# Order of the passes over a split weight granule: both passes on the high half first, those on the low half last

## The chip, the cores and the metric

The kernel runs on one core of one Trainium2 chip. The metric is device time in microseconds (us), median of several runs. TensorE (PE, with its weight loads PEld), VectorE (DVE), ScalarE (ACT), GpSimd (POOL) and SyncE (SP, which here only issues DMAs) each work through a queue of their own and wait for each other by semaphores.

## The reference, cut to what matters

One decoder layer on 512 tokens of width 2048, all in float32. The large matrix products are `h @ w_in` (2048 x 6160), `o @ w_o` (2048 x 2048), the FFN's up projection `h @ w_ffn_in` (2048 x 11264) and its down projection (5632 x 2048):

```python
h = rmsnorm(x, attn_pre_norm[l])
m = token_mixer(h, w_in[l], ...)          # proj = h @ w_in; GLA heads and differential attention; o @ w_o
x = x + rmsnorm(m, attn_post_norm[l])
h = rmsnorm(x, ffn_pre_norm[l])
f = conv_ffn(h, w_ffn_in[l], ...)         # up = h @ w_ffn_in; (gelu(conv(a)) * b) @ w_ffn_out
x = x + rmsnorm(f, ffn_post_norm[l])
```

## The kernel before

**Split operands.** Each operand X of a large product is held as two tiles of a reduced type: a high half (`hi`, X rounded by an ACT copy) and a low half (`lo` = X - hi, a DVE subtraction). A product is then three matmuls: high tokens by high weights, low tokens by high weights, high tokens by low weights. Token halves lie in `ah` and `al` (or in `in_s2h`, `in_s2l` and the like for sums of token blocks).

**Granules.** Weights come in granules of 128 x 1024 elements: a DMA brings one into a buffer (`raw` or `rt`, four of each; `wt`), ACT writes the high half (line 137), DVE the low half (line 138), each into one of three slots of `ring` (some granules go to other tiles, `xhi` and `xlo`, or to `w`). A granule feeds 24 matmuls with 256 columns or 12 with 512 columns. The high slot is written again when the last matmul that reads it is done, and so is the low slot; the buffer is loaded again when the DVE subtraction is done.

**Stages.** In order of time: the boot with the first input projection (`first_half`, then `proj_n` and `proj_t`); the mixer, whose input projections run in `InUnit`, with the matmuls of the heads (GLA and attention, plain float32, made by generators that `step()` moves on) between granules; the output projection (`proj_n`, `to_ffn`); the up projection (`up_prods`, in units of seven block products after a Strassen-like scheme); the down projection (`down_prods`, ten units, each of seven block products of two granules); and the last group of 512 rows (`last_group`, `ffn_out_part`).

- `mm_n` (lines 191 to 193): one token tile by two slices of a granule; tokens are loaded as the stationary operand, weights move (512 columns). It is called for four token tiles in turn per granule.
- `InUnit.run` (lines 742 to 744 and 746 to 748): either weights are stationary and tokens move (`turned`), or the other way round; 256 columns.
- `down_prods` (lines 1349 to 1351): token sums stationary, weights move, 512 columns, two banks `b[0]` and `b[1]` for the two token tiles. When a block product is done, `into` adds each bank to `acc` (line 1357, DVE; line 1355, ACT, for a first one). The same banks are written on by a later block product.
- `ffn_out_part` (lines 1553 to 1555), in the last group; `mm_t` (lines 173 to 175) and `up_prods` (lines 1247 to 1249) have moving tokens and stay as they are.

**What sets the order.** In `first_half`, `to_ffn`, `run_in_order` (the change from up to down projection) and the end of `last_group` PE, ACT, DVE and POOL run in the order of the code. Elsewhere a list scheduler, which plays the program through with a model of time, sets the order of each engine, DMA queues included. So a change in the order of PE's code can move other engines' instructions there.

In a down unit the weights of three blocks are loaded from memory, others are made from them: `more` (line 1195, POOL) adds a second block to a buffer by an accumulating DMA, and lines 1212 and 1230 (DVE) add one buffer to another. Token sums are loaded into `st` and split by lines 150 and 151.

## Time and profile before

| | |
|---|---|
| median of 3 runs | 2100.62 us (2098.62 to 2102.5) |
| the profiled execution's own time | 2097.49 us |
| its span, first to last instruction | 2095.8 us |
| mean granted TensorE clock | 0.998 |
| DVE busy | 1509.7 us, 72% of the span |
| ACT busy | 1002.5 us, 48% |
| POOL busy | 286.3 us, 14% |
| DMA, mean | 171 GB/s |

In the profile's rows `L1350 PE MATMUL bank<-ring,ah` names line, engine, operation, and output and inputs (moving operand first). A row of waits reads: engine, tile and line that waited, what it waited for, then the time in total, how often, and the longest one. A matmul's end is modelled, so that matmuls that follow each other overlap in the rows: their rate is read from the starts.

### The profile page before, as it was taken

What the parts mean: (1) busy time and instruction counts of PE and PEld (TensorE: products, weight loads), DVE (VectorE), ACT (ScalarE), POOL (GpSimd) and SP (SyncE); (2) the same over time, 40 slices, a digit from 0 to 9 for tenths busy, and PEclk for the clock granted to TensorE, in tenths of its full rate; (3) what the DMA queues carried; (4) which work ended last, traced back from release to release, by engine and by line L of the source; (5) the groups of instructions that cost most, each with busy time, mean ns of one, the idle gap of its engine ahead of it and who ended that gap; (6) DMA issues with size and microseconds to landing.
All of it is one profiled execution on the core that took longest, in us unless ns stands there. A gap on an engine that the chain in (4) does not pass through costs nothing.

```text
span 2095.8 us, 35570 instructions
## 1 busy us (share of the span) xinstructions
PE 2059.0 (98%) x14449; PEld 1900.7 (91%) x14449; DVE 1509.7 (72%) x1802; ACT 1002.5 (48%) x1306; POOL 286.3 (14%) x306
## 2 busy tenths in 40 slices
PE   7999999999999999999999999999999999999997
PEld 6699999999988889899999999999999878787786
DVE  5967777676762255976777777777777778888877
ACT  5544444455742233454554554555455554444443
POOL 0112222322200000011011111110111110110100
PEclk9999999999999999999999999999999999999999
DMA  5488887878884344447667577667766876776763
GB/s 210 121 186 182 193 193 177 180 176 196 197 229 151 96 159 151 138 107 192 153 150 192 144 162 186 142 160 173 167 157 181 240 211 166 189 195 159 175 166 141
DMA packets 280696, 358.60 MB, mean 171 GB/s; under 512 B 14592, under 2 KB 221876, under 8 KB 278612
## 3 DMA queue, kind: packets, MB, share of 16 engines
q1 hardware_dynamic: 191380, 259.85, 37.2%
q0 software_dynamic: 84800, 94.38, 29.7%
q8 instruction: 113, 1.85, 0.4%
q10 hardware_dynamic: 4352, 2.10, 0.3%
q14 instruction: 51, 0.42, 0.1%
HBM read 311.72 MB, written 44.56 MB: 170 GB/s over the span
## 4 chain that ended last, share of the span: by engine, by line
PE 60%; issue 30%; DMA 3%; DVE 3%; POOL 3%; ACT 1%; SPq 0%; POOLq 0%; DVEq 0%; ACTq 0%
PE bank L1247 6%; PE bank L1248 6%; PE bank L1249 6%; PE bank L192 3%; PE bank L193 3%; PE bank L191 3%; PE bank L742 3%; PE bank L744 3%; PE bank L743 3%; PE bank L746 3%; PE bank L748 3%; PE bank L747 3%; PE bank L173 2%; PE bank L175 2%; PE bank L174 2%
## 5 line engine op out<-in xcount | busy, mean ns | idle before, releaser
L138 DVE TENSOR_TENSOR ring<-raw,ring 128x1024 fp32r<-128x1024 f32 x315 | 383.4, 1222 | 281.0 <-ACT ring L137 271.1
L137 ACT ACTIVATE ring<-raw 128x1024 fp32r<-128x1024 f32 x315 | 333.2, 1060 | 509.2 <-PE bank L1248 113.9
L1247 PE MATMUL bank<-ah,ring 128*128 128x256 f32 x1280 | 353.4, 276 | 0.0
L1248 PE MATMUL bank<-al,ring 128*128 128x256 f32 x1280 | 353.4, 276 | 0.0
L1249 PE MATMUL bank<-ah,ring 128*128 128x256 f32 x1280 | 353.4, 276 | 0.0
L137 ACT ACTIVATE ring<-rt 128x1024 fp32r<-128x1024 f32 x221 | 233.4, 1060 | 247.8 <-PE bank L1248 154.9
L138 DVE TENSOR_TENSOR ring<-rt,ring 128x1024 fp32r<-128x1024 f32 x221 | 269.1, 1221 | 86.9 <-ACT ring L137 86.7
L1247 PEld LDWEIGHTS bank<-ah,ring 128*128 128x128 f32 x1280 | 240.3, 188 | 0.1
L1248 PEld LDWEIGHTS bank<-al,ring 128*128 128x128 f32 x1280 | 240.3, 188 | 0.1
L1249 PEld LDWEIGHTS bank<-ah,ring 128*128 128x128 f32 x1280 | 240.3, 188 | 0.0
L1350 PE MATMUL bank<-ring,ah 128*128 128x512 f32 x424 | 166.2, 392 | 6.3 <-DVE ring L138 6.3
L1351 PE MATMUL bank<-ring,al 128*128 128x512 f32 x424 | 165.1, 389 | 0.0
L1349 PE MATMUL bank<-ring,ah 128*128 128x512 f32 x424 | 158.3, 391 | 0.0
L192 PE MATMUL bank<-ring,ah 128*128 128x512 f32 x280 | 110.0, 394 | 0.6 <-DVE ring L138 0.6
L191 PE MATMUL bank<-ring,ah 128*128 128x512 f32 x280 | 109.6, 397 | 0.0
L193 PE MATMUL bank<-ring,al 128*128 128x512 f32 x280 | 109.3, 393 | 0.0
L1195 POOL DMA_DIRECT2D raw<-in_w_ffn_in_dram x40 | 51.2, 1309 | 395.5 <-DVE ring L138 395.5
L1350 PEld LDWEIGHTS bank<-ring,ah 128*128 128x128 f32 x424 | 79.6, 188 | 26.1 <-DVE ring L138 9.9
L1349 PEld LDWEIGHTS bank<-ring,ah 128*128 128x128 f32 x424 | 79.5, 188 | 18.1 <-ACT ring L137 1.4
L1195 POOL DMA_DIRECT2D rt<-in_w_ffn_in_dram x40 | 50.9, 1271 | 326.9 <-DVE ring L138 292.4
L1351 PEld LDWEIGHTS bank<-ring,al 128*128 128x128 f32 x424 | 79.6, 188 | 16.3
L746 PE MATMUL bank<-ring,ah 128*128 128x256 f32 x320 | 92.7, 290 | 1.7 <-ACT ring L137 1.0
(346 smaller groups left out, 5670.9 us busy)
## 6 DMA issues: line engine op xcount, KB each, us to landing
raw<-in_w_ffn_in_dram SPq DMA_DIRECT2D x96, 512.0 KB, 5.0
raw<-in_w_in_dram SPq DMA_DIRECT2D x56, 512.0 KB, 4.8
raw<-in_w_ffn_out_dram SPq DMA_DIRECT2D x48, 512.0 KB, 6.2
raw<-in_w_in_dram POOLq DMA_DIRECT2D x40, 512.0 KB, 7.1
rt<-in_w_ffn_in_dram SPq DMA_DIRECT2D x40, 512.0 KB, 5.6
rt<-in_w_ffn_in_dram POOLq DMA_DIRECT2D x40, 512.0 KB, 6.1
raw<-in_w_ffn_in_dram POOLq DMA_DIRECT2D x40, 512.0 KB, 6.8
raw<-in_w_o_dram SPq DMA_DIRECT2D x32, 512.0 KB, 3.9
```

The source lines that it names most:

```text
L137: act(hi, raw, AF.Copy)
L138: tt(lo, raw, hi.bitcast(F32), ALU.subtract)
L191: mm(banks[t], ah[:, t, s, :], w[0][:, k, :], start=st, stop=False)
L192: mm(banks[t], ah[:, t, s, :], w[1][:, k, :], start=False, stop=False)
L193: mm(banks[t], al[:, t, s, :], w[0][:, k, :], start=False, stop=sp)
L746: mm(o, sh[:, n, kk, :], wh[:, k, :], start=st, stop=False, **NOW)
L1247: mm(o, wh, sh[:, :, kk, :], start=start and kk == 0 and n == 0, stop=False, **NOW)
L1248: mm(o, wh, sl[:, :, kk, :], start=False, stop=False, **NOW)
L1249: mm(o, wl, sh[:, :, kk, :], start=False, stop=kk == HK - 1, **NOW)
L1349: mm(b[j], sh[:, o:o + P], w[0][:, q, :], start=start and st == 0, stop=False, **NOW)
L1350: mm(b[j], sh[:, o:o + P], w[1][:, q, :], start=False, stop=False, **NOW)
L1351: mm(b[j], sl[:, o:o + P], w[0][:, q, :], start=False, stop=st == 3, **NOW)
```

## The change

Within each granule, all matmuls that read the high half of the weights come first, and those that read the low half last. Before, the three products of one slice followed each other. This is done in `InUnit.run`, in `down_prods`, in `ffn_out_part` and in `mm_n`; in `mm_n` within the six matmuls of one token tile only. The matmuls themselves, their number, operands and banks stay the same.

```diff
     def mm_n(banks, t, g, w, slots=tuple(range(KT))):
-        for k in range(2):
+        for v, p, k in ((ah, 0, 0), (al, 0, 0), (ah, 0, 1), (al, 0, 1), (ah, 1, 0), (ah, 1, 1)):
             i = 2 * g + k
-            st, sp, s = i == 0, i == KT - 1, slots[i]
-            mm(banks[t], ah[:, t, s, :], w[0][:, k, :], start=st, stop=False)
-            mm(banks[t], ah[:, t, s, :], w[1][:, k, :], start=False, stop=False)
-            mm(banks[t], al[:, t, s, :], w[0][:, k, :], start=False, stop=sp)
+            mm(banks[t], v[:, t, slots[i], :], w[p][:, k, :], start=i == 0 and p == 0 and v is ah,
+               stop=i == KT - 1 and p == 1)
...
                 wh, wl = granule(None, 4, raws[g])
-                for n in range(2):
-                    o = b[:, 256 * n:256 * (n + 1)]
-                    for k in range(4):
-                        kk = 4 * g + k
...
-                            mm(o2, ch, sh[:, :, kk, :], start=st, stop=False, **NOW)
-                            mm(o2, ch, sl[:, :, kk, :], start=False, stop=False, **NOW)
-                            mm(o2, cl, sh[:, :, kk, :], start=False, stop=sp_, **NOW)
-                        else:
-                            mm(o, sh[:, n, kk, :], wh[:, k, :], start=st, stop=False, **NOW)
-                            mm(o, sl[:, n, kk, :], wh[:, k, :], start=False, stop=False, **NOW)
-                            mm(o, sh[:, n, kk, :], wl[:, k, :], start=False, stop=sp_, **NOW)
+                for w in (wh, wl):
+                    for n in range(2):
+                        o = b[:, 256 * n:256 * (n + 1)]
+                        for k in range(4):
+                            kk = 4 * g + k
...
+                                mm(o2, cw, sh[:, :, kk, :], start=st, stop=sp_, **NOW)
+                                if w is wh:
+                                    mm(o2, cw, sl[:, :, kk, :], start=False, stop=False, **NOW)
+                            else:
+                                mm(o, sh[:, n, kk, :], w[:, k, :], start=st, stop=sp_, **NOW)
+                                if w is wh:
+                                    mm(o, sl[:, n, kk, :], w[:, k, :], start=False, stop=False, **NOW)
...
     def down_prods(b, op, g, w, start):
         sh, sl = (piece(v, *place[op]) for v in (ah, al))
-        for j in range(2):
-            for q in range(2):
-                o = 512 * g + 256 * q + P * j
-                st = 2 * g + q
-                mm(b[j], sh[:, o:o + P], w[0][:, q, :], start=start and st == 0, stop=False, **NOW)
-                mm(b[j], sh[:, o:o + P], w[1][:, q, :], start=False, stop=False, **NOW)
-                mm(b[j], sl[:, o:o + P], w[0][:, q, :], start=False, stop=st == 3, **NOW)
+        for p in range(2):
+            for j in range(2):
+                for q in range(2):
+                    o = 512 * g + 256 * q + P * j
+                    st = 2 * g + q
+                    mm(b[j], sh[:, o:o + P], w[p][:, q, :], start=start and st == 0 and p == 0,
+                       stop=st == 3 and p == 1, **NOW)
+                    if p == 0:
+                        mm(b[j], sl[:, o:o + P], w[0][:, q, :], start=False, stop=False, **NOW)
...
     def ffn_out_part(us, gr, t, c):
         b = bank()
-        for k in range(4):
...
-            mm(b, uh[:, tk], hi[:, k % 2, :], start=k == 0, stop=False)
-            mm(b, uh[:, tk], lo[:, k % 2, :], start=False, stop=False)
-            mm(b, ul[:, tk], hi[:, k % 2, :], start=False, stop=k == 3)
+        for v, p, k in [(v, 0, k) for k in range(4) for v in range(2)] + [(0, 1, k) for k in range(4)]:
+            mm(b, us[k][v][:, tk], gr[k // 2][p][:, k % 2, :], start=(v, p, k) == (0, 0, 0),
+               stop=(p, k) == (1, 3))
```

Lines 195 to 730 of the kernel before stand two lines higher in the changed one, `into` two lines lower, `ffn_out_part` and what follows one line higher.

**PE, one granule of a down unit.** Before (in square brackets the engine whose semaphore the instruction waits for; ACT writes the high half, DVE the low one):

```order
L1349 MATMUL bank<-ring,ah 128x512 [waits Activation_49]
L1350 MATMUL bank<-ring,ah 128x512 [waits DVE_49]
L1351 MATMUL bank<-ring,al 128x512
L1349 MATMUL bank<-ring,ah 128x512
L1350 MATMUL bank<-ring,ah 128x512
L1351 MATMUL bank<-ring,al 128x512
L1349 MATMUL bank<-ring,ah 128x512
L1350 MATMUL bank<-ring,ah 128x512
L1351 MATMUL bank<-ring,al 128x512
L1349 MATMUL bank<-ring,ah 128x512
L1350 MATMUL bank<-ring,ah 128x512
L1351 MATMUL bank<-ring,al 128x512
```

And in the changed kernel, where line 1350 multiplies high tokens (by either half of the weights) and line 1353 low tokens:

```order
L1350 MATMUL bank<-ring,ah 128x512 [waits Activation_49]
L1353 MATMUL bank<-ring,al 128x512
L1350 MATMUL bank<-ring,ah 128x512
L1353 MATMUL bank<-ring,al 128x512
L1350 MATMUL bank<-ring,ah 128x512
L1353 MATMUL bank<-ring,al 128x512
L1350 MATMUL bank<-ring,ah 128x512
L1353 MATMUL bank<-ring,al 128x512
L1350 MATMUL bank<-ring,ah 128x512 [waits DVE_49]
L1350 MATMUL bank<-ring,ah 128x512 x3
```

The wait for DVE's low half moved from the second matmul of the granule to the ninth; the twelve matmuls are the same.

**DVE in a down unit**, where the scheduler sets the order: line 138 is a low half of weights, line 151 a low half of token sums, line 1357 (1359 in the changed kernel) adds a finished bank to `acc`. Before:

```order
L151 TENSOR_TENSOR al<-st,ah 128x1024
L138 TENSOR_TENSOR ring<-raw,ring 128x1024 x2
L1357 TENSOR_TENSOR acc_16858<-acc_16858,bank 128x512
L1357 TENSOR_TENSOR acc_16859<-acc_16859,bank 128x512
L151 TENSOR_TENSOR al<-st,ah 128x1024
L138 TENSOR_TENSOR xlo<-raw,xhi 128x1024
```

And in the changed kernel:

```order
L138 TENSOR_TENSOR ring<-raw,ring 128x1024
L151 TENSOR_TENSOR al<-st,ah 128x1024
L138 TENSOR_TENSOR ring<-raw,ring 128x1024
L1359 TENSOR_TENSOR acc_16858<-acc_16858,bank 128x512
L1359 TENSOR_TENSOR acc_16859<-acc_16859,bank 128x512
L138 TENSOR_TENSOR xlo<-raw,xhi 128x1024
L151 TENSOR_TENSOR al<-st,ah 128x1024
```

A low half of weights moved ahead of the low half of token sums that stood before it.

**SP, which issues the loads**, at the change from one group of down units to the next (before with -, changed with +; `st` are token sums, `raw` and `rt` weights):

```order
-L102 DMA raw<-in_w_ffn_out_dram 128x2x512
+L102 DMA raw<-in_w_ffn_out_dram 128x2x512 x2
 L48 DMA st<-sd2a_8344 128x1024
 L102 DMA raw<-in_w_ffn_out_dram 128x2x512 x2
 L48 DMA st<-sd3a_8349 128x1024
-L102 DMA raw<-in_w_ffn_out_dram 128x2x512
 L48 DMA st<-sd3s_8352 128x1024
-L48 DMA rt<-in_w_ffn_out_dram 128x2x512
+L48 DMA rt<-in_w_ffn_out_dram 128x2x512 x2
 L48 DMA st<-sd3s_8353 128x1024
-L48 DMA rt<-in_w_ffn_out_dram 128x2x512
```

The weight loads `raw` and `rt` each stand one load of token sums earlier than before.

In the mixer too DVE, ACT and, in a few places, SP and POOL have a changed order of the heads' work against the weight splits. In the up projection, up to the change to the down projection, no engine's order is changed.

13 lines of the change are left out of this document (6 added, 7 removed).

## The prediction

> **What bounds the kernel now.** I read the clock first, then the page's busy shares, the list of waits of PE, and the stages.
>
> ```profile
> core 0: 2095.8 us, clock 0.998
> PE 2059.0 (98%) x14449; PEld 1900.7 (91%) x14449; DVE 1509.7 (72%) x1802; ACT 1002.5 (48%) x1306; POOL 286.3 (14%) x306
> ```
>
> PE is busy for 98% of the span at full clock. Its matmuls are neither fewer nor smaller afterwards, so the change can win only some of the 36.8 us in which PE is idle, plus what the modelled ends hide. The list of PE's waits says which part:
>
> ```profile
> PE bank L158 <- DVE xt L247: 10.4, 2, 9.5
> PE bank L1350 <- DVE ring L138: 6.3, 8, 1.0
> PE bank L1350 <- DVE xlo L138: 1.6, 3, 0.8
> PE bank L646 <- ACT aT L639: 1.3, 1, 1.3
> PE bank L646 <- DMA dvt<-dvd: 1.0, 1, 1.0
> PE bank L746 <- ACT ring L137: 1.0, 1, 1.0
> PE bank L175 <- DVE xlo L138: 0.8, 1, 0.8
> PE bank L1554 <- DVE xlo L138: 0.8, 1, 0.8
> PE bank L748 <- DVE ring L138: 0.8, 1, 0.8
> PE bank L192 <- DVE ring L138: 0.6, 1, 0.6
> ```
>
> Every row with `L138` is PE waiting for a low half. Except for L175, which the change leaves alone, they are matmuls that read the low half: L1350 (down projection, 11 times, 7.9 us), L1554, L748 and L192 (once each). The 10.4 us of L158 are the boot's wait for scaled tokens. PE meets its low half almost at once after the high one; in the timeline of the down stage:
>
> ```profile
> 1820.37 0.39 PE L1351 MATMUL bank<-ring,al 128*128 128x512 f32 x1
> 1820.59 0.62 PE L1349 MATMUL bank<-ring,ah 128*128 128x512 f32 x2
> 1822.24 0.50 PE L1350 MATMUL bank<-ring,ah 128*128 128x512 f32 x1 [1.03 <-DVE ring L138]
> 1822.58 0.39 PE L1351 MATMUL bank<-ring,al 128*128 128x512 f32 x1
> ```
>
> From start to start a 512-column matmul takes 0.22 us (1820.37 to 1820.59), so the second of the two L1349 began at about 1820.82, and the low half was 1.2 us late (1822.24 less 1820.82, less 0.22).
>
> **The change, part by part.**
>
> *Down projection, the wait for the low half.* How much later may the low half come? Before, it is the second matmul of a granule, afterwards the ninth: seven matmuls of 0.227 us, 1.6 us later. The longest wait listed for it is 1.0 us, the one above 1.2 us by its starts. So all 11 waits should go. What each is worth is more than its listed idle time, since the modelled end covers a part. A second place, with the cause in view (PE, ACT and DVE):
>
> ```profile
> 1692.36 0.39 PE L1351 MATMUL bank<-xhi,al 128*128 128x512 f32 x1
> 1692.62 0.50 PE L1349 MATMUL bank<-ring,ah 128*128 128x512 f32 x1
> 1693.88 0.50 PE L1350 MATMUL bank<-ring,ah 128*128 128x512 f32 x1 [0.76 <-DVE ring L138]
> 1694.22 0.39 PE L1351 MATMUL bank<-ring,al 128*128 128x512 f32 x1
> 1696.61 0.51 PE L1349 MATMUL bank<-ring,ah 128*128 128x512 f32 x1
> 1697.86 0.50 PE L1350 MATMUL bank<-ring,ah 128*128 128x512 f32 x1 [0.75 <-DVE ring L138]
> ...
> 1691.50 1.06 ACT L137 ACTIVATE ring<-rt 128x1024 fp32r<-128x1024 f32 x1 [8.48 <-PE bank L1351]
> 1695.49 2.01 ACT L137 ACTIVATE ring<-rt 128x1024 fp32r<-128x1024 f32 x2 [1.01 <-DMA rt<-in_w_ffn_out_dram]
> ...
> 1692.60 1.23 DVE L138 TENSOR_TENSOR ring<-rt,ring 128x1024 fp32r<-128x1024 f32 x1 [5.30 <-ACT ring L137]
> ```
>
> L1349 to L1350 takes 1.26 us in place of 0.23, and the next step 0.34: 1.14 us lost where 0.76 us of idle time is listed. In the first example it is 1.2 + 0.1 for 1.03. With 0.3 us more for each, the 11 waits are worth 7.9 + 11 x 0.3 = 11.2 us.
>
> Not all of it stays won, since the high half is late here too: ACT begins when the accumulating DMA into `rt` lands, ends at 1692.56, and PE begins at 1692.62. The granule behind it starts at 1696.61, 0.33 us after its predecessor, again right behind its own high half. That DMA is issued once, so when the first of the pair loses its 1.1 us stall, PE reaches the second 1.1 us earlier and waits for the high half. I take 1.0 us off for this pair. The other pairs that I see in the timeline lie several granules apart, and there the load chain begins with a ring slot that PE frees, so it moves with PE. The weight loads name the granules in which the high half is just in time:
>
> ```profile
> PEld bank L1350 <- DVE ring L138: 9.9, 10, 1.5
> PEld bank L1350 <- DVE xlo L138: 3.1, 4, 1.1
> PEld bank L1349 <- ACT ring L137: 1.4, 4, 0.5
> ```
>
> Four granules. The low slot is now read by the twelfth matmul, not by the eleventh, so DVE gets it back 0.23 us later, and with it comes the next load of that buffer: 4 x 0.23 = 0.9 us off. The high slot comes free four matmuls (0.9 us) earlier, which I count as nothing, since ACT is busy for less than half of the time. Down projection: 11.2 - 1.0 - 0.9 = 9.3 us.
>
> *The two banks.* The first bank's last matmul moves from sixth to tenth of the last granule, 0.9 us later; the second bank still ends with the twelfth. DVE adds the two to `acc` one behind the other, and stands still if it comes too early, with the next low half behind it.
>
> ```profile
> L1357 DVE TENSOR_TENSOR acc<-acc,bank 128x512 f32<-128x512 f32 x124 | 80.8, 679 | 3.1 <-PE bank L1351 3.1
> 1645.00:2035.00 390.00, 382.03 (x1688) 311.89 (x1687) 322.44 (x341) 182.20 (x190) 44.97 (x38) 1.00 0.71 188
> ```
>
> In 124 such additions DVE waited for PE for 3.1 us in all, so it nearly always comes after both banks are done. If it comes exactly when the second is done less its 0.68 us for the first, the first may now hold it by 0.23 us (0.68 less two matmuls). DVE has 390 - 322 = 68 us free in this stage. I cost it at nothing; the cover is the 1.6 us that a low half may now be late. If it is gone, see the second rival.
>
> *Order of DVE and SP.* Weight halves go ahead of token halves on DVE (one operation, 1.22 us by the row of 1692.60), and the weight loads one `st` load earlier on SP. The latter bears on the late high halves, since SP is a queue:
>
> ```profile
> SPq L48 <- DVE al L151: 155.1, 35, 13.1
> ```
>
> A load of token sums that waits for its buffer holds the weights behind it. I see no granule whose lateness this row proves, so I take nothing; at best the late high halves go (1.9 us more), at worst a token half comes 1.22 us later and PE waits for it. No wait of PE above names `al` of L151; were token halves late as often as weights are (11 waits in 10 units of 14 granules), 35 splits would give 3 waits of 1.1 us, 3 us.
>
> *Last group, mixer, projections.* L1554: 0.8 + 0.3 = 1.1 us; the low half may be 1.6 us later, so it goes. L748: the low half moves from third to seventeenth of 24 matmuls of 0.113 us, 1.6 us later, so 0.8 + 0.2 = 1.0 us goes; L746, which waited 1.0 us for the high half right before it, stays. L192: `mm_n` orders only its own six matmuls, so the low half is allowed just 3 x 0.227 = 0.7 us more, against 0.6 + 0.3 = 0.9 us: I take 0.7.
>
> *The reordered mixer.* The scheduler moves the heads' work among the weight splits. Where PE idles there:
>
> ```profile
> 400.00:620.00 220.00, 214.63 (x1654) 202.94 (x1653) 154.21 (x285) 130.29 (x246) 43.67 (x55) 0.99 0.81 192
> ```
>
> 5.4 us, of which 1.0 is L746 and 0.8 L748. Of the other 3.6 us, 2.3 are attention's (L646). No row shows what the new order does to it; I bound it by all 3.6 us gone and by the 5.4 us doubled, and take 0, because the same work fills the same gaps.
>
> *Reloading weights.* The loads show whether the order of operands on PE matters by itself:
>
> ```profile
> L1350 PEld LDWEIGHTS bank<-ring,ah 128*128 128x128 f32 x424 | 79.6, 188 | 26.1 <-DVE ring L138 9.9
> L1351 PEld LDWEIGHTS bank<-ring,al 128*128 128x128 f32 x424 | 79.6, 188 | 16.3
> ```
>
> Before, L1349 and L1350 mostly use the same stationary tile in turn; afterwards they don't. The row of L1350 has a load of 188 ns for each of its matmuls, as L1351, whose tile is new each time. So nothing is saved before, and nothing lost after: 0. The Trainium skill ("TensorE: Matmul & The Clock Gate", section "Step-by-step: what each phase is for") says that loading and multiplying are separate so that one can load once and multiply repeatedly; by that rule this change would give up reuse. The trace doesn't agree that any is had here (188 ns on both rows).
>
> *Sum.* 9.3 + 1.1 + 1.0 + 0.7 = 12.1 us off the profiled execution: 2097.5 (span 2095.8 and 1.7 around it) less 12.1 is 2085.4. That execution lies 3.1 us under the median of the runs, 2100.6, so the forecast as a median is 2088.5 us.
>
> **The rivals.**
>
> *The stalls move to the high half (no change).* Every late granule is late because its buffer landed late, and PE, coming earlier, waits on L137 in place of L138. For it speaks the pair at 1692 and 1696; against it, that only four weight loads waited for a high half, and that ACT elsewhere is ahead by whole granules: in the first example it was DVE that was behind. Then only L1554, L748 and the second half of L192's stay won, about 2.5 us: 2098 us.
>
> *DVE held by the banks (slower).* At the end of each of the 70 block products of the down projection DVE stands 0.23 us longer before the first bank, and the low halves behind it come late by more than their 1.6 us. It decides once DVE's backlog eats that cover, so if DVE comes to the additions early. The price is 70 x 0.23 = 16 us at the most, and the 11.2 us of stalls stay as they are: 2100.6 - 2.8 (the other places) + 16 = 2114 at worst, and half of it 2106. Against it: 3.1 us of such waits in all, 68 us of free time.
>
> *The mixer's new order costs (less gain).* The doubled 5.4 us against the sum: 2094 us.
>
> *Reuse lost.* If a matmul whose stationary tile is the one before's needed no load of its own, 560 pairs in the down projection (10 units x 14 granules x 4) would each get one more load of 188 ns, all of it exposed at worst: 105 us, 2088.5 + 105 = 2194 us. The equal 188 ns rows leave it 1 in 100. (It is the rule of the Trainium skill's page named above.)
>
> **How the numbers follow.** Chances: the forecast, with the stalls gone (2083 to 2092), 0.64; the mixer's loss or part of the stalls moved (2092 to 2096), 0.15; stalls moved whole (2097 to 2100), 0.14; slower, 0.07, of which 0.06 is DVE held and 0.01 reuse. The lower end of the range is the forecast with the mixer's 3.6 us and the late high halves' 1.9 us won too: 2088.5 - 5.5 = 2083. The upper end takes in the moved stalls: 2100. A measurement tells about 0.2%, 4.2 us, from no change, so faster is below 2096.4: 0.79; within 0.2%: 0.14; slower: 0.07.
>
> **What would show it.** Right: no waits for DVE in the down stage's matmuls (lines 1350 and 1353 then), nor in the last group's or the mixer's L746 to L748; PE's busy time unchanged at the same rate of 0.227 and 0.113 us; idle time of PE below 25 us. A high half in place of the low one in the list of waits (ACT L137 or its DMA) would show the first rival, additions to `acc` that wait for PE the second, weight loads of other than 188 ns the last. The forecast is wrong if the gain of the down stage is under 5 us, or if the mixer's stretch from 400 to 620 us moves by more than 5 us.

## The result, and the profile after

The changed kernel is slower: 2109.74 us in the median of 5 runs (2105.51 to 2111.13) against 2100.62 us (5 runs, 2098.62 to 2104.17). The ratio is 1.0039, with a 95% interval of 1.0023 to 1.0054: 8 us more (5 to 11), where 12 us less were forecast. Both signs by which the forecast was to be called wrong came true: the down stage gained less than 5 us, and the mixer moved by more. The profiled execution took 2109.98 us:

```profile
core 0: 2108.3 us, clock 0.996
```

```profile
PE 2063.5 (98%) x14449; PEld 1906.8 (90%) x14449; DVE 1507.1 (71%) x1802; ACT 999.7 (47%) x1306; POOL 281.4 (13%) x306
```

The work is the same (14449 matmuls), the span 12.5 us longer than in the trace of before, which was one of its quicker executions. Rows of the list of PE's waits, as in the prediction (engine, tile and line, what it waited for, us in total, times, longest), show what came in place of the waits for low halves; in the changed lines the list has none of these any more:

```profile
PE bank L1350 <- DVE acc L1359: 6.5, 6, 2.5
PE bank L833 <- DVE p L821: 5.2, 1, 5.2
PE bank L1350 <- ACT ring L137: 2.6, 3, 1.8
PE bank L644 <- ACT aT L637: 2.5, 3, 1.4
PE bank L1249 <- DVE ring L138: 1.3, 2, 0.8
PE bank L173 <- ACT gv L855: 1.2, 1, 1.2
```

In the down projection (L1350) PE now waits 9.1 us, 6.5 of them for the additions of finished banks to `acc` and 2.6 for high halves; before it waited 7.9 us, all for low halves. In the mixer two waits appear or grow: L833, the transposes of the gated block, for the gate's product (L821), and L644 (L646 before), attention, for `aT`. L173, which the change leaves alone, waits 1.2 us for a copy on ACT. L1249 lies in the up projection, which the change leaves alone too; such waits come and go there from trace to trace (from its first matmul to the down projection's it takes 756.2 to 761.9 us in the traces in which nothing of it is changed).

By the first matmuls of the stages in the two traces, the changed kernel is 9.5 us later when the up projection begins (894.6 against 885.2 us), 11.6 us later when the down projection begins, and 12.5 us later when the last group begins. So nearly all is lost in the mixer, and the down projection takes 394.8 us where it took 393.9 (392.9 to 397.3 us in eight further traces with its order of before): its gain of 9 us didn't come at all. The two stretches that the prediction quoted (PE, PEld, DVE, ACT, POOL busy; clock, DMA share, GB/s):

```profile
400.00:620.00 220.00, 210.76 (x1614) 199.58 (x1613) 148.05 (x277) 125.48 (x236) 44.27 (x55) 0.98 0.80 188
1645.00:2035.00 390.00, 380.94 (x1720) 313.93 (x1720) 323.47 (x340) 181.57 (x191) 47.34 (x40) 1.00 0.71 184
```

**Waits in the down projection.** In five of the six waits for additions (4.0 of the 6.5 us) DVE goes from one operation to the next without a pause, and the addition that PE waits for stands behind additions of buffers, token splits and weight splits. In the timeline (start, length, engine, line, and in brackets the idle time before and its releaser):

```profile
1755.08 1.22 DVE L1230 TENSOR_TENSOR rt<-rt,raw 128x1024 f32<-128x1024 f32 x1
1756.21 1.22 DVE L138 TENSOR_TENSOR ring<-raw,ring 128x1024 fp32r<-128x1024 f32 x1
1757.35 1.28 DVE L1359 TENSOR_TENSOR acc<-acc,bank 128x512 f32<-128x512 f32 x2
1758.17 0.47 PE L1350 MATMUL bank<-ring,ah 128*128 128x512 f32 x1 [0.60 <-DVE acc L1359]
```

The longest wait, 2.5 us at 1977, is of another kind: DVE itself stood idle, since the addition was behind a token split whose load had landed late.

```profile
1972.73 1.06 ACT L150 ACTIVATE ah<-st 128x1024 fp32r<-128x1024 f32 x1 [4.97 <-DMA st<-ud]
1973.83 1.23 DVE L151 TENSOR_TENSOR al<-st,ah 128x1024 fp32r<-128x1024 f32 x1 [2.86 <-ACT ah L150]
```

**The wait at the end of the mixer.** ACT splits `dt`, which landed late, and only then does the sigmoid (L820) on which DVE's product L821 and PE's transposes L833 depend:

```profile
610.66 0.63 ACT L150 ACTIVATE ah<-dt 128x512 fp32r<-128x512 f32 x1 [3.32 <-DMA dt<-dstd]
611.20 0.61 ACT L820 ACTIVATE p<-p 128x512 f32<-128x512 f32 x1
611.93 0.68 DVE L821 TENSOR_TENSOR p<-p,op 128x512 f32<-128x512 f32 x1
612.67 1.11 PE L833 MATMUL bank<-ident,p 128*128 128x128 f32 x4 [5.17 <-DVE p L821]
```

Not all of the 5.2 us is loss. Counted by PE's work (the n-th matmul of one trace against the n-th of the other), the changed kernel is 2.6 us behind at 540 us of the time of before, 5.8 at 595, ahead of this block, and 9.4 at 616, behind it: 3.6 us are lost here, since before PE had waited 1.7 us a little earlier, for a high and a low half, and had then run at half the clock (last section). At 540 us ten more traces with the mixer of before lie between 1.8 us ahead of it and 0.6 us behind.

**The wait in the first gate unit.** In the changed kernel a weight split that waits for its load stands ahead of the table load and the sigmoid on ACT; the copy `aT`, which PE's attention needs, comes behind all of them:

```profile
541.41 1.06 ACT L137 ACTIVATE ring<-raw 128x1024 fp32r<-128x1024 f32 x1 [3.38 <-DMA raw<-in_w_in_dram]
542.49 1.28 ACT L820 ACT_TABLE_LOAD   x1
543.78 0.63 ACT L820 ACTIVATE u<-u 128x512 f32<-128x512 f32 x1
546.66 0.48 ACT L637 ACTIVATE aT<-bank 128x384 f32<-128x384 f32 x1
547.20 1.56 PE L644 MATMUL bank<-dvt,aT 128*128 128x256 f32 x6 [1.35 <-ACT aT L637]
```

Before, the sigmoid came first, and `aT` was 2.2 us earlier:

```profile
538.21 0.63 ACT L820 ACTIVATE u<-u 128x512 f32<-128x512 f32 x1
540.20 1.06 ACT L137 ACTIVATE ring<-raw 128x1024 fp32r<-128x1024 f32 x1 [1.36 <-DMA raw<-in_w_in_dram]
544.41 0.47 ACT L639 ACTIVATE aT<-bank 128x384 f32<-128x384 f32 x1
```

But the changed kernel is 2.6 us behind by then, so the same matmul waits for `aT` about as long as before (1.35 us for 1.30): in the whole change this place costs nothing. It does where PE comes to it earlier (e6, e13 and e17 below).

### The profile page after: what moved, and what is told of

Same layout as the page of the kernel before. It is cut to its first block, busy times and chain, and to the rows that moved or that the text cites. A ratio compares the mean times of both kernels' runs of the same rounds, so it can differ in the third digit from the quotient of the medians.

```text
span 2108.3 us, 35612 instructions
## 1 busy us (share of the span) xinstructions
PE 2063.5 (98%) x14449; PEld 1906.8 (90%) x14449; DVE 1507.1 (71%) x1802; ACT 999.7 (47%) x1306; POOL 281.4 (13%) x306
## 4 chain that ended last, share of the span: by engine, by line
PE 53%; issue 34%; DMA 4%; POOL 3%; DVE 3%; ACT 1%; POOLq 0%; SPq 0%; DVEq 0%; ACTq 0%
PE bank L190 10%; PE bank L742 6%; PE bank L746 5%; PE bank L1247 4%; PE bank L1249 4%; PE bank L1248 4%; PE bank L744 3%; PE bank L748 3%; PE bank L1350 2%; PE bank L175 2%; PE bank L173 2%; PE bank L174 2%; POOL raw L1195 1%; PE bank L1553 1%; POOL rt L1195 1%
## 5 line engine op out<-in xcount | busy, mean ns | idle before, releaser
L138 DVE TENSOR_TENSOR ring<-raw,ring 128x1024 fp32r<-128x1024 f32 x315 | 383.1, 1221 | 290.3 <-ACT ring L137 287.3
L137 ACT ACTIVATE ring<-raw 128x1024 fp32r<-128x1024 f32 x315 | 333.1, 1061 | 531.4 <-PE bank L1248 112.4
L1249 PE MATMUL bank<-ah,ring 128*128 128x256 f32 x1280 | 353.4, 276 | 0.8 <-DVE ring L138 0.8
L1247 PE MATMUL bank<-ah,ring 128*128 128x256 f32 x1280 | 353.3, 276 | 0.0
L137 ACT ACTIVATE ring<-rt 128x1024 fp32r<-128x1024 f32 x221 | 232.7, 1059 | 249.7 <-PE bank L1248 141.5
L138 DVE TENSOR_TENSOR ring<-rt,ring 128x1024 fp32r<-128x1024 f32 x221 | 269.0, 1221 | 87.9 <-ACT ring L137 86.3
L1350 PE MATMUL bank<-ring,ah 128*128 128x512 f32 x848 | 270.8, 392 | 9.1 <-DVE acc L1359 6.5
L1249 PEld LDWEIGHTS bank<-ah,ring 128*128 128x128 f32 x1280 | 240.3, 188 | 1.0 <-DVE ring L138 1.0
L1247 PEld LDWEIGHTS bank<-ah,ring 128*128 128x128 f32 x1280 | 240.3, 188 | 0.1
L1350 PEld LDWEIGHTS bank<-ring,ah 128*128 128x128 f32 x848 | 159.9, 189 | 46.5 <-ACT ring L137 6.2
L190 PE MATMUL bank<-ring,ah 128*128 128x512 f32 x560 | 177.2, 395 | 0.2 <-ACT ah L150 0.2
L190 PEld LDWEIGHTS bank<-ring,ah 128*128 128x128 f32 x560 | 106.2, 190 | 22.5 <-ACT ah L150 0.6
L746 PE MATMUL bank<-ring,ah 128*128 128x256 f32 x640 | 118.0, 283 | 0.4 <-ACT ring L137 0.4
L742 PE MATMUL bank<-ah,ring 128*128 128x256 f32 x640 | 117.6, 282 | 0.0
L746 PEld LDWEIGHTS bank<-ring,ah 128*128 128x128 f32 x640 | 99.4, 189 | 1.3 <-ACT ring L137 0.6
L742 PEld LDWEIGHTS bank<-ah,ring 128*128 128x128 f32 x640 | 99.2, 188 | 0.1
```

The lines of the kernel that those rows point to most:

```text
L137: act(hi, raw, AF.Copy)
L138: tt(lo, raw, hi.bitcast(F32), ALU.subtract)
L190: mm(banks[t], v[:, t, slots[i], :], w[p][:, k, :], start=i == 0 and p == 0 and v is ah, stop=i == KT - 1 and p == 1)
L742: mm(o2, cw, sh[:, :, kk, :], start=st, stop=sp_, **NOW)
L746: mm(o, sh[:, n, kk, :], w[:, k, :], start=st, stop=sp_, **NOW)
L1247: mm(o, wh, sh[:, :, kk, :], start=start and kk == 0 and n == 0, stop=False, **NOW)
```

## The experiments

Theory A at the start: the time is lost in the mixer through the order that the scheduler gives the other engines, and the down projection's gain is eaten by the additions that stand later on DVE. All ratios are against runs of the kernel before on the same chip (medians of 2099.1 to 2100.8 us), with their 95% intervals; 0.001 is 2.1 us.

### Which part costs

**e1, the change of `down_prods` alone.** (The hunk of `down_prods` of the change, nothing else.)

> Only the down projection has the changed order; the mixer, `mm_n` and the last group are as before. Theory A (the time is lost in the mixer, where the scheduler's new order makes PE wait for the heads; the down projection's own gain is eaten by waits for the additions to `acc`): 2098 to 2102 us, no wait of L1350 or L1353 for L138, but about 6 us of waits of L1350 for the additions (DVE, `acc`). The prediction's theory (each place brings its own gain): 2091 us, no waits for additions. A third theory (the down projection itself is what got slower): over 2105 us.

Measured: 2099.75 us, ratio 1.0001 (0.9989 to 1.0013). As theory A has it: no wait for a low half in the stage, and

```profile
PE bank L1350 <- DVE acc L1359: 6.1, 5, 1.9
PE bank L1350 <- ACT ring L137: 3.8, 3, 1.9
```

9.9 us of other waits for the 7.9 us that went.

**e2, the change of `InUnit.run` alone.**

> Only `InUnit.run` has the changed order. Theory A: 2108 to 2112 us, with PE waiting some 5 us for the gate product (L833 for DVE L821) at the end of the mixer and more than 2 us for attention (L646), and the down projection's 11 waits for the low half there as before. The prediction's theory: 2099.6 us. If the loss needs both parts together: about 2100 us.

Measured: 2109.79 us, ratio 1.0043 (1.0027 to 1.0060). It is the whole loss:

```profile
PE bank L835 <- DVE p L823: 4.8, 1, 4.8
```

(L835 and L823 are L833 and L821 of the other kernels. Attention, L646, waits 2.8 us for `aT`; in traces with the mixer of before that is 0.9 to 2.0 us.) The parts in `mm_n` and `ffn_out_part` weren't tried alone; e1 and e2 together leave nothing for them to explain.

### Where in the mixer

The mixer has ten units; the last two are the gate units (`gate_unit`). These kernels choose the order by unit or block product:

```diff
+            self.nr = InUnit.count
...
+                tri = ((0, 0), (0, 1), (1, 0))
+                if self.nr < 8:   # e5;  e6 and e12: self.nr >= 8
+                    todo = [(p, v, n, k) for p in range(2) for n in range(2) for k in range(4) for v in range(2 - p)]
+                else:
+                    todo = [(p, v, n, k) for n in range(2) for k in range(4) for p, v in tri]
+                for p, v, n, k in todo:
...
```

(p is the half of the weights, v that of the tokens.) **e5, the first eight units:**

> Of the ten mixer units the first eight have the changed order; the last two (the gate units) and everything behind them are as before. Theory A (most of the loss arises in the gate units, where ACT splits `dt`, loaded late, ahead of the sigmoid L820 that the transposes L833 need): no wait of PE for the gate product L821, and 2102 to 2104 us, the rest being some 2.5 us of slower spacing of the 256-column matmuls in the turned units. Rival (the changed order costs something in every granule of the mixer): 8/10 of the loss, 2107 to 2108 us.

**e6, the last two units:**

> Only the last two of the ten mixer units (the gate units) have the changed order. Theory A: the wait for the gate product L821 is there with some 5 us, and waits for attention; 2105 to 2107 us. Rival (a cost in every granule): 2102 us, no such wait.

Measured: e5 2101.03 us, ratio 1.0001 (0.9992 to 1.0011); its list has neither a wait of L835 nor one of L646. e6 2108.03 us, ratio 1.0031 (1.0019 to 1.0043), a fifth of the granules with most of the loss:

```profile
PE bank L835 <- DVE p L823: 5.0, 1, 5.0
PE bank L646 <- ACT aT L639: 3.3, 2, 2.7
```

So a cost of the same size in every granule is excluded, and the gate units are the place of most of the loss.

**e12, the same with the splits of `dt` on POOL,** so that neither ACT nor DVE stands behind them:

```diff
-            split(*(v[...] for v in (ah, al)), u...)
+            nc.gpsimd.tensor_copy(hi, src)
+            nc.gpsimd.tensor_tensor(lo, src, hi.bitcast(F32), ALU.subtract)
```

> The changed order in the last two mixer units only, as in the run of those alone, and the splits of `dt` (8, each behind a late DMA) run on POOL, so that neither ACT nor DVE can stand behind them; on both, the gate's operations are in the same places otherwise. Theory A (the wait for the gate product comes from the splits of `dt` that the scheduler put ahead of L820 on ACT and of L821 on DVE): the wait falls from 5 us to 1 to 3, and the time from 2108 to 2103 to 2105 us. Rival (the chain of the gate is that long by itself): still 5 us and 2107 to 2109 us.

```profile
PE bank L835 <- DVE p L823: 3.5, 1, 3.5
```

Measured: 2105.65 us, ratio 1.0028 (1.0016 to 1.0041). The wait fell by 1.5 us, a little less than expected, and the time can't be told from that of e6. The `dt` splits are a minor part. What is left can be read from the traces: DVE's chain from L784 to L823 (L782 to L821 before) has one weight split more in it, and its last operation starts 4.1 us after its first for 3.1 before; and PE makes up 3.7 us on its way to L835 (by its work 5.0 us behind at 595 us, 1.3 at 608), since it has no half to wait for there and no half clock behind it. No run separates the two.

**e13 and e14, the gate units without their last three block products, and those three alone** (conditions `self.nr >= 8 and not (self.nr == 9 and seg in ("x1", "y1", "y2"))`, and the inner one):

> The changed order in the last two mixer units, except in the last three block products (x1, y1, y2 of the last unit), so in 17 of 20... block products of two granules there are 14 in two units, and 11 of them are changed. ACT's order at the gates' end is the same as before. Theory A (the loss comes from the order of ACT, DVE and SP at that end): 2100 to 2102 us, waits for L821 of at most 1 us. Rival (late low halves in every granule of the gate units cost something): 11/14 of the loss, 2105 to 2107 us.

> The changed order only in the last three block products of the mixer (six granules). On ACT the gate's sigmoid L820 then stands behind one more weight split, as in the whole change, but not behind a split of `dt`; SP keeps its order. Theory A: a part of the wait for L821, 1 to 3 us, and 2102 to 2104 us. Rival (low halves on PE late in the last granules are enough): 5 us of wait and 2106 to 2108 us.

Measured: e13 2105.12 us, ratio 1.0022 (1.0013 to 1.0031); e14 2100.80 us, 1.0008 (0.9998 to 1.0017). Theory A expected it the other way round for e13, and falls as to the place: the greater part, some 4.6 us, is lost ahead of the last block products. e13's time is that of its rival, by which low halves cost something in every granule; e18 below speaks against it. In e13 one long wait of attention's, in the first gate unit, carries the loss. In e14 the gate's product is waited for, but the time can't be told from that of before:

```profile
PE bank L646 <- ACT aT L639: 4.6, 1, 4.6
```

```profile
PE bank L835 <- DVE p L823: 2.8, 1, 2.8
```

**e17 and e18, to tell ACT's order from late low halves in the first gate unit.** Theory B: the split ahead of the sigmoid on ACT is the cause. With z1 and x1 changed (e17) the scheduler moves it; with all but x1 changed (e18) it does not (both are seen in the traces):

```diff
+                if self.nr == 8 and seg in ("z1", "x1"):   # e17;  e18: self.nr == 8 and seg != "x1"
```

> The changed order only in two of the seven block products (z1 and x1) of the first gate unit, 96 of 3360 matmuls of the mixer. The scheduler then puts a weight split (L137, behind a load) ahead of the table load and the sigmoid L820 on ACT, as in the whole change, and exchanges two weight loads on SP. Theory B (this order on ACT is what makes PE wait for aT): the wait for aT (L646) of 1.3 us becomes 3 to 5 us, and 2103 to 2105 us. Rival (the loss grows with the number of granules whose low half is read late): under 1 us of loss, about 2100 us.

> The changed order in the six other block products of the first gate unit (all but x1), 288 matmuls. ACT has the sigmoid ahead of the weight split there, as before, and SP's order is that of before altogether. Theory B: no loss at that place, 2099 to 2101.5 us, the wait for aT at 1 to 2 us. Rival (late low halves cost something in every granule): three times the loss of the run with two block products, 2103 us or more.

```profile
PE bank L646 <- ACT aT L639: 3.8, 1, 3.8
```

```profile
PE bank L646 <- ACT aT L639: 3.6, 2, 2.9
```

Measured: e17 2101.02 us, ratio 1.0011 (1.0001 to 1.0021); e18 2099.74 us, 1.0006 (0.9997 to 1.0016). e17 stays under the 2103 us that theory B gave it as the least, e18 under the 2103 us of its rival, and the intervals of the two overlap; late low halves in six block products cost at most 3.4 us (0.0016). By PE's work in the two traces, e17 loses 4.2 us between 540 and 555 us and e18 1.7; ten traces with the mixer of before spread from 0.4 gained to 2.9 lost there, so e17 alone stands out. The traces favour theory B, but attention's wait grew in e18 too, and the times don't show it: what exactly in the order around the first gate unit costs how much stays open.

### Where the down projection's gain went

**e3, each bank finished by itself, and e4, only the last two matmuls of each triple exchanged:**

```diff
+        for p, v, j, q in [(p, v, j, q) for j in range(2) for p, v, q in
+                           ((0, 0, 0), (0, 1, 0), (0, 0, 1), (0, 1, 1), (1, 0, 0), (1, 0, 1))]:   # e3
+        for p, v, j, q in [(p, v, j, q) for j in range(2) for q in range(2)
+                           for p, v in ((0, 0), (0, 1), (1, 0))]:   # e4
```

> Only the down projection is changed, and each bank is finished by itself: its four passes on the high half, then its two on the low half, then the same for the second bank. The low half is read by the fifth matmul (0.7 us later than before, not 1.6), and the first bank ends with the sixth as before. Here the additions stand later on DVE in 14 places of 124, where the whole change has 22. Theory A with the order on DVE as cause of the new waits: additions awaited for under 3 us in all, low halves for 1 to 2 us: 2092 to 2096 us. If the new waits come from granules whose high half is late anyway: waits for ACT L137 instead, and 2099 to 2102 us.

> Only the down projection is changed, and in each triple only the last two matmuls change places, so that the low half is read by the third matmul in place of the second (0.23 us later). DVE, ACT, SP and POOL have the same order as in the kernel that finishes each bank by itself, so the difference of the two is the price of the low half's lateness alone. Theory A: 11 waits of 0.2 us less each, 2097 to 2100 us, and 3 to 5 us slower than the kernel that finishes each bank by itself. If the moved order of DVE is harmful in itself: slower than before, over 2101 us. If the order on DVE alone brings the gain: as fast as that kernel.

Measured: e3 2100.90 us, ratio 1.0008 (0.9998 to 1.0019); e4 2100.28 us, 0.9998 (0.9988 to 1.0008). Both expectations of theory A miss: no gain in either. (The orders of the two differ in the traces after all, in five places on DVE; ACT's and POOL's are the same.) The waits of e3 and of e4, in the rows that answer to e1's:

```profile
PE bank L1350 <- ACT ring L137: 3.7, 3, 1.6
PE bank L1350 <- DVE acc L1356: 3.1, 3, 1.5
```

```profile
PE bank L1350 <- DVE ring L138: 3.5, 8, 0.5
PE bank L1350 <- DVE acc L1356: 2.1, 2, 1.5
```

With the remaining rows (L138 and `xhi` in e3, L137 and `xlo` in e4) the stage has 8.5 us of waits in e3 and 8.2 us in e4, after 7.9 before, 9.1 in the whole change and 9.9 in e1. What PE waits for is another thing each time, and how long it waits is nearly the same. So it would look if one engine behind all of these things were late: DVE makes the low halves, adds the banks, frees buffers for loads.

**e7, DVE relieved, the order of before:** the additions of one weight buffer to another cover 128 of 1024 columns, which leaves out most of these sums. It covers all 114 of them, 36 in the down projection (0.29 us each for 1.22, 33 us less there) and the others in the up projection.

```diff
-                tt(self.t[g], self.t[g], self.b22[g], ALU.add)
+                n = 128 if self.joined else GR   # joined: the units of the up and down projections
+                tt(self.t[g][:, :n], self.t[g][:, :n], self.b22[g][:, :n], ALU.add)   # and so with b21
```

> The order of before everywhere. In the down units the additions of one weight buffer to another (lines 1212 and 1230) cover 128 of 1024 columns, so that DVE has some 1.0 us less for each of 36 of them, about 40 us less in this stage, with the same dependencies; the sums are left out for the other columns, so the output is another one. Theory A (in the down stage DVE, in order and near its limit in every second unit, is what comes late, and PE waits for whatever it does last): most of the 11 waits for the low half go, 2090 to 2094 us. Rival (the latency of the loads sets the lateness, not DVE): 2098 to 2101 us, with the waits for the low half as before.

**e8, the same with the changed order in the down projection:**

> The same narrow additions with the changed order in the down projection alone. Theory A: with DVE relieved the waits for the additions to `acc` go too, 2088 to 2092 us, and the changed order is worth up to 4 us beside the kernel with narrow additions and the order of before. Rival (latency of the loads): waits for ACT L137, whose buffer lands late, stay or grow, 2097 to 2100 us, no difference between the two orders.

Measured: e7 2090.83 us (2090.14 to 2091.99), ratio 0.9953 (0.9941 to 0.9966); e8 2089.66 us (2088.87 to 2091.48), 0.9947 (0.9935 to 0.9960). A row of e7's waits, one of e8's, and the group of e8's additions to `acc`:

```profile
PE bank L1352 <- DVE ring L138: 2.6, 4, 0.8
```

```profile
PE bank L1352 <- ACT ring L137: 2.9, 3, 1.8
```

```profile
L1361 DVE TENSOR_TENSOR acc<-acc,bank 128x512 f32<-128x512 f32 x124 | 79.6, 683 | 27.9 <-PE bank L1352 27.9
```

With DVE relieved 10 us come off with either order, in the down projection: from its first matmul to the last group's it takes 386.4 us (e8: 385.9) for 393.9, or 392.9 to 397.3 in the other traces with the order of before. In e8 no addition is waited for any more; the additions wait for PE instead (27.9 us in the last row). The changed order adds 1.2 us, within the spread.

Which waits went? Of the 11 of before, three (2.9 us, at 1822, 1901 and 1978) have DVE busy without a pause, behind additions of buffers and a token split. Four more (2.3 us, at 1721, 1738, 1815 and 1894) follow an idle DVE: an accumulating DMA had just landed, and the high half was late as well. One of each kind, from the trace of before:

```profile
1819.84 1.22 DVE L151 TENSOR_TENSOR al<-st,ah 128x1024 fp32r<-128x1024 f32 x1
1820.97 1.22 DVE L138 TENSOR_TENSOR ring<-rt,ring 128x1024 fp32r<-128x1024 f32 x1
```

```profile
1813.97 1.23 DVE L138 TENSOR_TENSOR xlo<-rt,xhi 128x1024 fp32r<-128x1024 f32 x1 [2.11 <-ACT xhi L137]
```

These seven are gone in e7. The other four (2.7 us, up to 1698) lie in the first unit, where e7 takes nothing off DVE (the unit's own four additions keep their width), and they stay: they are the four of e7's row. In e8 waits for high halves come in their place there, as long in all (2.9 us).

So theory A holds for the stage behind its first unit: DVE sets the time, directly or through the loads (POOL issues an accumulating DMA when DVE is done with the buffer), and a longer leeway for one of its products only changes which product PE waits for. Not separated in e7 is that a narrow addition also brings its own sum 0.9 us earlier. For the first unit no run shows what sets the time.

**Attempts to have that with nothing left out.** e9 and e10 run those additions on POOL (order of before, changed order in the down projection), e11 runs the token sums' low halves on POOL with the changed order there, e15 and e16 make the 18 additions of line 1230 in the down units by accumulating DMAs (order of before, changed order).

```diff
-                tt(self.t[g], self.t[g], self.b22[g], ALU.add)
+                (nc.gpsimd.tensor_tensor if self.joined else tt)(self.t[g], self.t[g], self.b22[g], ALU.add)   # e9, e10; and so with b21
...
-        split(piece(ah, *place[n]), piece(al, *place[n]), raw)
+        act(piece(ah, *place[n]), raw, AF.Copy)   # e11
+        nc.gpsimd.tensor_tensor(piece(al, *place[n]), raw, piece(ah, *place[n]).bitcast(F32), ALU.subtract)
...
+                    nc.gpsimd.dma_start(out=self.t[g]..., in_=self.block(1, 0, g), accum_op=ALU.add)   # e15, e16, in x1
```

> The order of before everywhere; nothing is left out. The additions of one weight buffer to another (lines 1212 and 1230, 114 in the up and down projections) run on POOL in place of DVE. That takes 1.2 us off DVE for each. How long POOL needs isn't in the traces so far; its 128x512 selections take 0.8 us, so I estimate 1.6 to 2.5 us for 1024 columns, in front of a high half that waits for it. Theory A (DVE is what comes late in the down stage): most waits for the low half go, 2091 to 2096 us. Rival (what DVE gains is lost since the sum now comes later, or since POOL issues the accumulating DMAs later): 2099 us or more, with waits of PE for ACT L137.

> The same additions on POOL, with the changed order in the down projection alone; nothing is left out. Theory A: as with the order of before, and 1 to 4 us faster, since a low half may be later here: 2088 to 2094 us, no waits for additions to `acc`. Rival (the order does not matter once DVE is relieved): within 1 us of the kernel with the order of before. Rival (POOL's sums come late): 2099 us or more.

> The changed order in the down projection alone, and the low halves of the token sums of this stage (line 151 on `st`, some 30 operations in every second unit) on POOL in place of DVE; nothing is left out. These stood ahead of late additions to `acc` in DVE's queue. Theory A: the waits for additions fall from 6 us to under 2, and the time to 2092 to 2097 us. Rival (POOL is slower and holds the accumulating DMAs, or PE waits for the token halves): 2099 us or more, with waits for `al`.

> The order of before everywhere, nothing left out. In the down units 18 of the 36 additions of one weight buffer to another (line 1230) are made by an accumulating DMA that reads the block a second time, as other blocks are added already. DVE has 18 x 1.22 = 22 us less in this stage, POOL 18 issues of 1.2 us more, the DMA queues 9.4 MB more. Theory A (DVE late): two thirds of what the narrow additions gave, -5 to -7 us, 2093 to 2096 us. Rival (the longer way of the sum, or POOL's queue, eats it): 2099 to 2103 us with waits for ACT L137.

> The same accumulating DMAs with the changed order in the down projection alone; nothing left out. Theory A: the waits for additions to `acc` fall from 6 us to under 3, and the time is that with the order of before or up to 2 us less, 2091 to 2096 us. Rival: 2099 us or more, with waits for ACT L137 of more than 4 us.

Measured: e9 2206.57 us, ratio 1.0509 (1.0490 to 1.0527); e10 2211.79, 1.0540 (1.0525 to 1.0554); e11 2122.58, 1.0109 (1.0096 to 1.0123); e15 2105.85, 1.0031 (1.0019 to 1.0043); e16 2106.78, 1.0038 (1.0024 to 1.0052). All are slower than theory A had it, and the kernel of before is beaten by no version that computes everything. In e9 an addition takes 2.7 (L1212) to 3.1 us on POOL, and DVE's own additions get slower beside it (0.68 us before, in the list of groups):

```profile
L1230 POOL TENSOR_TENSOR rt<-rt,raw 128x1024 f32<-128x1024 f32 x56 | 172.2, 3074 | 70.3 <-DVE ring L138 64.5 <-DVE xlo L138 5.8
L1322 DVE TENSOR_TENSOR s<-u 128x512 f32<-128x512 f32 x20 | 48.2, 2411 | 3.7 <-DMA sd2s<-s 0.8 <-DMA sd3s<-s 0.8 <-DMA sd1s<-s 0.7
```

The Trainium skill says of this ("Advanced Engine Details and Errata", section "GPSIMD Details") that POOL shares a read and a write interface with DVE, with conflicts where DVE has two SBUF inputs; L1322 and the rows of L138, which went from 1.22 to 1.40 us on `rt`, have two, and agree. In e15 the DMA share of the stage rises from 0.71 to 0.82, and the waits for low halves in the down projection are longer than before (10.0 us for 7.9), though DVE has less to do:

```profile
1645.00:2035.00 390.00, 378.27 (x1660) 306.18 (x1659) 296.36 (x314) 177.31 (x187) 67.29 (x57) 1.00 0.82 203
```

Whether there the further transfers or POOL's longer queue (67 us busy for 45) delay the loads wasn't separated.

## Why the prediction was wrong, point by point

- *Down projection, the wait for the low half.* Right as a mechanism: none of the 11 waits is left, in the change and in e1. Wrong as a gain: 9.3 us were counted, 0 came (e1: 1.0001). The sum took waits off one by one, as if each had a cause of its own. But seven of the 11 went with the work that e7 takes off DVE (10 us), and after the change DVE had no less to do. The prediction let the loads move with PE, because they begin with a ring slot that PE frees; but ahead of the 34 accumulating ones of the down units POOL waits 295 us in all, every time for DVE's split (L138).
- *The two banks.* Costed at nothing, since DVE had 68 us free in the stage and came after both banks. DVE is indeed never held by a bank now (3.1 us before, 0.0 in this row of the changed kernel), so the second rival as it was priced didn't happen:

```profile
L1359 DVE TENSOR_TENSOR acc<-acc,bank 128x512 f32<-128x512 f32 x124 | 79.3, 678 | 0.0
```

  What the step left out is that the scheduler sees the first bank ready later and takes another operation first: 22 of the 124 additions stand a place or two later on DVE, none earlier.
- *Order of DVE and SP.* This is the step that failed in the down projection. It took nothing and bounded the loss at 3 us, from token halves that come late. The additions weren't thought of as something that PE waits for. They cost 6.5 us of waits (6.1 in e1), 2.5 of these because a late token half stood ahead of one.
- *Stalls that move to the high half.* The pair was counted with 1.0 us. PE does wait there for the high half, for 1.8 us (2.6 us in all), and goes on at half the clock (below). With DVE relieved (e8) both granules of the pair wait for it, 2.8 us in all. The rival that moves all stalls to it was too narrow; the stalls moved, but to additions first.
- *The reordered mixer.* This is the step that failed by most. Taken as 0 "because the same work fills the same gaps", bounded by 5.4 us of loss. It lost 9.5 us between the traces and 9.0 us in e2 (0.0043 of 2100). Six to seven of these lie in the two gate units (e6), where PE waits for the gate's product and for attention's copies, which stand behind weight splits, a table load and a sigmoid on ACT. How much each of these costs stays open (e12 to e18). Its rival was named, with its price too small: PE's idle time there wasn't a measure of what the change can cost.
- *0.3 us more for each stall.* Not tested by itself. After two of the long ones (5.2 and 1.8 us) PE runs at half the clock for another 4.8 and 3.4 us, which costs 2.4 and 1.7 us more.
- *L748, L192, L1554* lost their waits for low halves as forecast (2.8 us in the sum), of which the last group gave 0.8 us back (L1553 waits 0.4 us each for an addition and a high half): from its first matmul on it takes 60.5 us before and after. (There the new order runs over two granules at once, so that the second high half is read two matmuls sooner than before.) The gains of the other two can't be read apart from the mixer's loss; *reloading* was rightly 0 (188 to 190 ns for each load after).

## What to carry to other kernels

A list of waits tells what an engine waited for last, not what would follow if that came earlier: before a wait is counted as won, ask which engine made it late, and whether that engine has to do less afterwards. If not, the wait goes to its next product; cutting that engine's work in a throwaway kernel (e7) tells this in one run. And where a scheduler orders the other engines, a change in one engine's order can be priced only by what moves in the others' queues too (e2: 9 us with the same instructions, though which move costs how much stayed open), first of all operations on which a chain hangs (a sigmoid behind a split that waits for a load), not by the idle time that was there before.

## What the runs showed of the hardware

After a pause PE's clock can fall to half, sooner than I had thought. In the changed kernel, the 5.1 us at the end of the mixer and the 3.4 us behind them (last columns: granted clock, DMA share, GB/s):

```profile
607.50:612.60 5.10, 0.00 (x1) 0.00 (x0) 4.14 (x7) 1.94 (x3) 0.00 (x0) 0.81 0.43 133
612.60:616.00 3.40, 3.33 (x17) 3.33 (x17) 3.40 (x6) 2.08 (x5) 0.00 (x0) 0.50 0.25 78
```

and the 4 us behind the wait of 1.8 us in the down projection:

```profile
1705.30:1709.30 4.00, 4.00 (x12) 3.13 (x13) 2.45 (x3) 1.13 (x2) 0.00 (x0) 0.63 0.43 139
```

Twelve matmuls began there, where 4 us hold 17 to 18 at 0.227 us, so this wait of 1.8 us costs nearly as much again. The kernel of before has such a stretch too, behind two waits of 0.97 and 0.76 us close to each other at the end of the mixer; and in the changed kernel the clock stays full behind the longest wait of the down projection, 2.5 us at 1977:

```profile
600.40:604.20 3.80, 3.75 (x19) 3.75 (x20) 3.77 (x6) 1.75 (x3) 0.00 (x0) 0.56 0.60 186
```

```profile
1977.00:1981.00 4.00, 4.00 (x18) 3.29 (x19) 4.00 (x5) 1.65 (x2) 0.00 (x0) 1.00 0.84 235
```

So the length of a pause alone doesn't decide. In each of the 20 traces (the boot left aside) the granted clock changes only at times that are whole multiples of 3.413 us apart, and it falls at the end of such a stretch in which PE had stood idle for about half of it: 1.5 us is the least idle time in a stretch with a fall behind it, 1.9 us the most without one. The wait of 1.8 us lies in one stretch (1702.93 to 1706.34), that of 2.5 us is cut in two by the end of one (1.6 and 0.9 us). The Trainium skill ("TensorE: Matmul & The Clock Gate", section "What's actually happening") has the clock fall after an idle window of about 3.4 us and rise after as long a busy one; the rise agrees (3.41 us at half clock from 1706.34 on), the fall does not, since 1.8 us of idle time were enough.

Matmuls of 256 columns follow each other by 113 ns in some granules and by about 118 ns in others, at the full clock and with nothing waiting. In 16 us of the same units of the mixer, before and after the change:

```profile
465.30:481.30 16.00, 16.00 (x143) 16.00 (x142) 8.22 (x7) 7.84 (x9) 5.10 (x4) 1.00 0.85 173
```

```profile
468.40:484.40 16.00, 16.00 (x138) 16.00 (x138) 7.35 (x6) 7.06 (x9) 5.08 (x4) 1.00 0.92 183
```

The changed order holds more of the turned units in the slower spacing: over the first eight units those that start within 0.13 us of each other do so by 116.3 ns in the mean for 114.7, which is 4 us for some 2540 of them, and in e2 and e5 it is the same. What sets it wasn't found, and e5, which has it, isn't measurably slower.
